# Planner costs for full fp32 products in the w_in stage, and two gMLP value blocks ahead of their inputs

## The chip, the cores and the metric

One NeuronCore of one Trainium2 chip runs the kernel. The metric is the device time of one execution in microseconds (us). TensorE is called PE, VectorE DVE, ScalarE ACT, GpSimd POOL; SP is the queue of SyncE, which issues nearly all DMAs here. An engine works through its own instructions strictly in the order of the program and waits at an instruction whose inputs are not there.

## What is computed

One layer over 640 tokens (512 latent, 128 context), model width 2048, all in fp32. Cut to what matters:

```python
h = rmsnorm(x, norm1_g) * (1.0 + sc1) + sh1
p = h @ w_in                                  # 2048 -> 3360 + 2048
o_a, s_fin = rwkv7_bidir(shift(p[..., :C_SHIFT]), s0)      # 8 pairs of heads
u, v = split(gelu(p[..., C_SHIFT:]), 2)       # gMLP, 8 groups of 128 channels
v = layernorm(v) * ln_g + ln_b                # per token and group
o_b = u * (w_spatial[g] @ v + b_spatial[g])   # per 128-token chunk
x = x + g1 * (concat(o_a, o_b) @ w_out)
# then: rmsnorm, SwiGLU (w_ffn_gate, w_ffn_up, w_ffn_down), final rmsnorm
```

## The kernel before

**The w_in stage** (some 150 to 1016 us of the profile) multiplies `h` by `w_in`, a block of 128 output channels at a time. A block has four pieces of 512 input channels, each split into two fp32r parts `hi` and `lo`, and takes 96 products of 128x128 by 128x320: the *wide* products, written as `big<-h_hi,hi`, `big<-h_lo,hi` and `big<-h_hi,lo`. What comes out of a block goes through a generator of its own: `take_r`, `take_v`, `take_k` for the pairs of heads, `take_gv` for a gMLP value block, `take_gu` for the gMLP gate block of the same group. These issue many *small* PE instructions: transposes, fp32 products on the whole array, and products on quarters or sixteenths of the array (64x64 and 32x32 modes), plus the `pm` products of the modulation (128x32 mode).

The order on every engine in this stage is a list written when the kernel is built. `Lister` keeps a clock for each engine, prices every instruction with a formula (`Op.__init__`, lines 106 to 130), and appends to each engine what its planned clock can start next; on PE it takes a small instruction when it has been ready long enough or two are ready, else the wide task (`pick`). The prices decide the order only; no wait is computed from them.

**Blocks and queues.** `block()` lines up the blocks pair by pair; the gMLP blocks are put behind the pairs by `GORD = (0, 1, 1, 2, 2, 3, 3, 8)`: groups 3 to 7 follow the last pair. All `take_gv` and `take_gu` generators stand in one queue, `qB`, and run one after the other.

**A value block** (`take_gv`, from line 946): gelu of 128x640, a transpose `pw` of `w_spatial`, five transposes `pvt`, then a chain on DVE, ACT and POOL: mean `gmn`, subtraction, square `gsq`, `gva`, `grs`, and three multiplications and additions on the tile `vt`. **A gate block** (`take_gu`): gelu (square and tanh on ACT in `gq`, three steps on DVE), five products `psp<-wspT,vt`, two additions `sp`, a last multiplication, and a store into `d_o`.

**The recurrence stage** follows (lines 1294 to 1580). Its order is set by the framework's scheduler, not by the list. It loads `gl` and `gr` (the gate's input), transposes tiles of `x` (`pxT<-ident,x1T`, two rounds per tile through one PSUM bank, each copied out by ACT), loads `o_b` back (`ol<-d_o`, cast to `oh`), multiplies it by half of `w_out` (`big<-oh,hi` and so on, called w_out products here), and runs the chunk recurrences of the pairs in between (`swap`, `w_ps`, `u_ps`, `s_ps`, `y_ps`). The single PSUM bank of the transposes is one that the w_in stage's last `psp` used.

Of the kernel before, what the change touches and what calls it, by code (L numbers as in the profile page):

```python
# [10 lines left out]
F32 = mybir.dt.float32  # L11
F32R = mybir.dt.float32r
# [7 lines left out]
P = 128  # L20
# [3 lines left out]
NT = T // P  # L24
# [7 lines left out]
DA = 1024  # L32
NPAIR = DA // P
CSH = 3360
# [16 lines left out]
TOGETHER = 2  # L51
PATIENCE = 2.0
SLACK = 1.0
NREC = 8
CHK = (3, 3, 4, 4, 4, 4)
POOLK = (3,)
# [32 lines left out]
class Op:  # L89
# [14 lines left out]
    def __init__(self, eng, name, fn, args, kw):  # L104
        ap = lambda x: hasattr(x, "tensor")
        self.eng, self.run = eng, lambda: fn(*args, **kw)  # L106
        outs = [x for x in (kw.get("out", args[0] if args else None), kw.get("accum_out")) if ap(x)]
        rest = [x for k, x in [*enumerate(args), *kw.items()] if ap(x) and not any(x is y for y in outs)]
        self.writes, self.reads = {x.tensor.name for x in outs}, {x.tensor.name for x in rest}
        self.stored = {x.tensor.name for x in outs if x.space == DRAM}  # L110
        n = max(math.prod(x.shape[1:]) for x in outs + rest)
        self.bytes, self.tiling = 0, None
        if name == "dma_start":
            run = min(self.run_of(x) for x in (outs[0], args[1]))
            self.bytes = 4 * math.prod(outs[0].shape) * min(4.0, max(1.0, 64 / run))
            self.cost = 0.5 if eng == "SP" else 0.65
        elif eng == "DVE":
            self.cost = 0.16 + 1e-3 * n * self.RATE.get(name, 1.03)
        elif eng == "ACT":
            self.cost = 0.2 + 0.83e-3 * n + 0.09 * any(ap(kw.get(k)) for k in ("scale", "bias"))  # L120
        elif eng == "POOL":
            self.cost = 0.05 + 1e-3 * n if name == "memset" else 0.2 + 0.185 * n
        else:
            lhs, rhs = args[1], args[2]
            q = lambda m: 32 if m <= 32 else 64 if m <= 64 else P
            self.tiling = (q(lhs.shape[0]), q(lhs.shape[1])) if name == "matmul" else (P, P)
            n = math.prod(rhs.shape[1:])
            share = P * P // (self.tiling[0] * self.tiling[1])
            least = {1: 0.108, 4: 0.05, 16: 0.016}[share] if self.tiling != (P, 32) else 0.08
            self.cost = max(least, (n / 2400 + 0.0133 if rhs.dtype == F32R else n / 1200) / share)  # L130


class Kept:
# [78 lines left out]


class Task:
    def __init__(self, gen, prio):
        self.gen, self.prio, self.item, self.over = gen, prio, None, False
        self.step()

    def step(self):
# [11 lines left out]
class Lister:  # L231
# [7 lines left out]
        self.wide = Task(wide, 0)  # L239
        self.tasks.append(self.wide)  # L240

    def add(self, gen, prio):
        self.tasks.append(Task(gen, prio))

    def ready(self, ops):
        e, r = ops[0].eng, 0.0
# [36 lines left out]
    def pick(self, eng, tasks):  # L283
        now = self.clock[eng]
        c = [(self.ready(t.item), t.rank(), i, t) for i, t in enumerate(tasks)]
        if eng == "PE":
            small = [x for x in c if x[3] is not self.wide and x[0] + SLACK * (x[3].item[0].tiling != self.tiling or self.tiling == (P, P)) <= now]
            wide = [x for x in c if x[3] is self.wide and x[0] <= now]
            full = [x for x in small if x[3].item[0].tiling == (P, P)]
            if full and self.tiling == (P, P):  # L290
                return now, min(full, key=lambda x: x[1])[3]
            if small and self.tiling != (P, P):
                same = [x for x in small if x[3].item[0].tiling == self.tiling]
                return now, min(same or small, key=lambda x: x[0])[3]
            if small and (not wide or len(small) >= TOGETHER or now - min(small)[0] >= PATIENCE):
                return now, min(small)[3]
            if wide:
                return now, self.wide
        start = min(max(now, x[0]) for x in c)
        return start, min((x for x in c if max(now, x[0]) <= start), key=lambda x: (x[1], x[0], x[2]))[3]  # L300
# [18 lines left out]
def flow_step(ctx: ExitStack, tc, x_prompt, x_sample, state_rwkv, c, c_ctx, w_mod, b_mod,  # L319
# [43 lines left out]
    def bcast(col, like):  # L363
        for _ in like.shape[2:]:
            col = col.unsqueeze(2)
        return col.to_broadcast(list(like.shape))
# [45 lines left out]
    wide = [0]  # L412
# [182 lines left out]
    bk, bp, gs, bz = (hp.enter_context(tc.tile_pool(name=n, bufs=1)) for n in ("bk", "bp", "gs", "bz"))  # L595
# [38 lines left out]
    class Mixer:  # L634


        def __init__(self):
            self.q, self.left, self.budget, self.done, self.apart = [], 0.0, 0.0, 0, False
            self.hold = 0

        def add(self, gen, cost):
            self.q.append(gen)
            self.left += cost
# [42 lines left out]
    bk, bp, gs, bz, db = Kept(bk), Kept(bp), Kept(gs), Kept(bz), Kept(db, 2)  # L686
# [163 lines left out]
    wl, done = {}, {"zv": 0}  # L850
# [85 lines left out]
    def gelu2(xx):  # L936

        sq = bp.tile([P, T], F32, tag="u2", name="gq", bufs=1)
        yield oS.activation(sq, xx, AF.Square)
        yield oV.tensor_scalar(sq, sq, GC1, 1.0, op0=ALU.mult, op1=ALU.add)  # L940
        yield oV.tensor_mul(sq, sq, xx)
        yield oS.activation(sq, sq, AF.Tanh, scale=GC0)
        yield oV.scalar_tensor_tensor(out=xx, in0=sq, scalar=1.0, in1=xx, op0=ALU.add, op1=ALU.mult)
# [3 lines left out]
    def take_gv(vv, g, read):  # L947
        lng, lnb, wsp = (gs.tile([P, P], F32, tag=n, name=n) for n in ("lng", "lnb", "wsp"))
        yield oQ.dma_start(lng, gmlp_ln_g[0, g].partition_broadcast(P))
        yield oQ.dma_start(lnb, gmlp_ln_b[0, g].partition_broadcast(P))  # L950
        yield oQ.dma_start(wsp, w_spatial[0, g])
        yield from gelu2(vv)
        yield slots.free
        pw = slots.tile([P, 4, P], F32, "pw")
        yield oT.transpose(pw[:, 0, :], wsp, ident)
        wspT = gs.tile([P, P], F32, name="wspT")
        yield oS.copy(wspT, pw[:, 0, :])
        slots.done(pw)
        vt = bp.tile([P, NT, P], F32, tag="vt2", name="vt2", bufs=1)
        yield from turned(vv, vt, "pvt2")  # L960
        bc = lambda ap: ap.unsqueeze(2).to_broadcast([P, NT, P])
        mn = gs.tile([P, NT], F32, name="gmn")
        yield oV.tensor_reduce(out=mn, in_=vt, axis=AX.X, op=ALU.add)
        yield oV.tensor_scalar_mul(mn, mn, 1.0 / P)
        yield oV.tensor_tensor(out=vt, in0=vt, in1=bc(mn), op=ALU.subtract)
        sq = bp.tile([P, NT, P], F32, tag="u2", name="gsq", bufs=1)
        yield oS.activation(sq, vt, AF.Square)
        va = gs.tile([P, NT], F32, name="gva")
        yield oV.tensor_reduce(out=va, in_=sq, axis=AX.X, op=ALU.add)
        yield oV.tensor_scalar(va, va, 1.0 / P, 4.0 * LN_EPS, op0=ALU.mult, op1=ALU.add)  # L970
        rstd = gs.tile([P, NT], F32, name="grs")
        yield oG.tensor_tensor(out=rstd, in0=va, in1=bcast(mhalf, va), op=ALU.pow)
        yield oV.tensor_tensor(out=vt, in0=vt, in1=bc(rstd), op=ALU.mult)
        fb = lambda ap: ap.unsqueeze(1).to_broadcast([P, NT, P])
        yield oV.tensor_tensor(out=vt, in0=vt, in1=fb(lng), op=ALU.mult)
        yield oV.tensor_tensor(out=vt, in0=vt, in1=fb(lnb), op=ALU.add)
        vts[g] = (vt, wspT)
# [149 lines left out]
    qA, qB, qS, qM, qT, qR, qX, qZ = [], [], [], [], [], [], [], []  # L1127
    blocks = [(FIRST[i], lambda h, read, i=i, n=n: low_rank(h, 24 + i, n), qA) for i, n in enumerate((P, P, 32))]

    def block(col, fn, i, q):  # L1130
        blocks.append((col, lambda pr, read: fn(pr, i, read), q))

    g = 0
    for p in range(NPAIR):
        block(P * p, take_r, p, qR)
        block(2 * DA + P * p, take_v, p, qR)
        block(DA + P * p, take_k, p, qA)
        while g < GORD[p]:
            block(CSH + DA + P * g, take_gv, g, qB)
            block(CSH + P * g, take_gu, g, qB)  # L1140
            g += 1
    pieces = [(b, q) for b in range(len(blocks)) for q in range(4)]
    N0 = 4 * len(FIRST)
    parts, praw = {}, []
# [150 lines left out]
    with ExitStack() as ph:  # L1295
# [26 lines left out]
        def flip(cc):  # L1322

            a, b = cc[0], NCH + cc[1]
            return slice(a, b + 1, b - a)
# [10 lines left out]
        def load_next():  # L1336
            if todo:
                _, p, ctx_, step = todo.pop(0)
                r = rw.tile([P, 2, REC], F32, tag="rec", name="rec", bufs=NREC)
                nc.sync.dma_start(r, d_S[p].rearrange("p d c f -> p (d c) f")[:, flip(seqs[ctx_][step])])  # L1340
# [207 lines left out]
        m3.run(4.0 + 8 * 4.0)  # L1548
        for _ in range(NREC - 4):
            load_next()  # L1550
# [26 lines left out]
    t1, t2 = slice(0, HALF), slice(HALF, T)  # L1577
# [629 lines left out]
```

## Time and profile before

| what | value |
|---|---|
| median of 3 runs | 3248.59 us (3248.25 to 3256.41) |
| the profiled execution | 3247.45 us; span of its instructions 3244.2 us |
| mean granted clock of TensorE | 0.983 |
| PE busy | 3107.5 us, 96% of the span |
| DVE, ACT, POOL busy | 72%, 45%, 39% |
| DMA | 553 MB moved, 170 GB/s over the span |

In the rows further down, a stretch is given as start:end and its length, then busy time and number of instructions of PE, PEld (weight loads, beside PE), DVE, ACT and POOL, the clock granted to TensorE as a share of its full speed, the mean busy share of the DMA engines and GB/s. A timeline row is start, duration, engine, line, operation, output<-input, shapes, how many, and in brackets the idle time of the engine before it and what ended that.

PE is the engine that is nearly always busy. The places where it stands still, or runs at half its clock, are where time can be won or lost.

### The profile page before, as it was taken

How to read it: one execution, taken by the hardware profiler on the slowest of the kernel's cores; microseconds unless marked ns; L12 is line 12 of the kernel's file. 1: busy time of each engine (PE TensorE's matmuls, PEld its weight loads, DVE VectorE, ACT ScalarE, POOL GpSimd, SP SyncE). 2: the span in 40 equal slices, each digit the busy share in tenths (PEclk: the TensorE clock that was granted, in tenths of full speed). 3: DMA queues.
4: the chain of work that ended last, by engine and by line, in shares of the span. 5: the costliest groups of instructions: out<-in, count | busy, mean ns of one | idle time of the engine just before them, and what ended most of it. 6: DMA issues, size and time to landing. Idle time of an engine off the chain costs nothing. (4 is left out here: it accounts for less than half of the span.)

```text
span 3244.2 us, 73519 instructions
## 1 busy us (share of the span) xinstructions
PE 3107.5 (96%) x28828; PEld 2877.5 (89%) x28828; DVE 2333.3 (72%) x4073; ACT 1446.0 (45%) x3161; POOL 1260.9 (39%) x1082
## 2 busy tenths in 40 slices
PE   5899999999998999898999999999999999999996
PEld 3698888889886877788999999999999999999986
DVE  4456767767666666547977877877877777777787
ACT  3244554555543333345644444444444444444365
POOL 0001222222220122301365666566666645555543
PEclk8899999999997999999999999999999999999998
DMA  8768788887896777455434434434433354554353
GB/s 319 254 183 237 212 224 212 237 233 192 230 233 191 215 222 226 136 152 175 123 108 130 125 105 128 127 107 123 123 116 118 110 180 151 160 160 141 110 170 119
DMA packets 741922, 553.00 MB, mean 170 GB/s; under 512 B 141688, under 2 KB 674184, under 8 KB 732744
## 3 DMA queue, kind: packets, MB, share of 16 engines
q1 hardware_dynamic: 729256, 534.62, 55.5%
q0 software_dynamic: 9984, 13.13, 1.7%
q8 instruction: 226, 3.70, 0.5%
q14 instruction: 120, 0.98, 0.1%
q10 hardware_dynamic: 2336, 0.57, 0.1%
HBM read 438.77 MB, written 111.69 MB: 170 GB/s over the span
## 5 line engine op out<-in xcount | busy, mean ns | idle before, releaser
L1819 PE MATMUL P<-xo,lo 128*128 128x320 f32 x2352 | 727.1, 309 | 3.5 <-DVE lo L1636 3.5
L1818 PE MATMUL P<-xo,hi 128*128 128x320 f32 x2352 | 727.6, 309 | 0.0
L1817 PE MATMUL P<-xo,hi 128*128 128x320 f32 x2352 | 727.6, 309 | 0.0
L1636 DVE TENSOR_TENSOR lo<-raw,hi 128x512 fp32r<-128x512 f32 x532 | 514.4, 974 | 162.0 <-ACT hi L1635 159.6
L1635 ACT CAST hi<-raw 128x512 fp32r<-128x512 f32 x532 | 330.2, 622 | 505.6 <-PE P L1818 435.6
L1819 PEld LDWEIGHTS P<-xo,lo 128*128 128x128 f32 x2352 | 441.6, 188 | 4.3 <-DVE lo L1636 4.2
L1818 PEld LDWEIGHTS P<-xo,hi 128*128 128x128 f32 x2352 | 442.3, 188 | 0.0
L1817 PEld LDWEIGHTS P<-xo,hi 128*128 128x128 f32 x2352 | 442.3, 188 | 0.0
L1730 POOL TENSOR_TENSOR raw<-raw 128x512 f32<-128x512 f32 x252 | 413.6, 1645 | 13.6 <-DVE lo L1636 0.6
L106 PE MATMUL big<-h_hi,hi 128*128 128x320 f32 x1280 | 417.8, 326 | 0.9 <-ACT praw L1209 0.9
L1819 PE MATMUL P<-xd,lo 128*128 128x320 f32 x1232 | 384.4, 312 | 16.8 <-DVE lo L1636 16.2
L106 PE MATMUL big<-h_lo,hi 128*128 128x320 f32 x1280 | 394.1, 308 | 0.0
L106 PE MATMUL big<-h_hi,lo 128*128 128x320 f32 x1280 | 394.1, 308 | 0.0
L1817 PE MATMUL P<-xd,hi 128*128 128x320 f32 x1232 | 381.9, 310 | 5.1 <-ACT hi L1635 3.0
L1818 PE MATMUL P<-xd,hi 128*128 128x320 f32 x1232 | 380.7, 309 | 0.0
L1730 POOL TENSOR_TENSOR t<-raw 128x512 f32<-128x512 f32 x84 | 129.5, 1542 | 454.8 <-DMA raw<-in_w_ffn_up_dram 407.5
L1635 ACT CAST hi<-rawd 128x512 fp32r<-128x512 f32 (+1 forms) x288 | 168.7, 588 | 237.9 <-PE P L1818 198.5
L106 PEld LDWEIGHTS big<-h_hi,hi 128*128 128x128 f32 x1280 | 240.7, 188 | 32.6 <-issue 25.9
L1819 PEld LDWEIGHTS P<-xd,lo 128*128 128x128 f32 x1232 | 231.2, 188 | 25.6 <-DVE lo L1636 25.6
L106 PEld LDWEIGHTS big<-h_lo,hi 128*128 128x128 f32 x1280 | 240.7, 188 | 1.2
L106 PEld LDWEIGHTS big<-h_hi,lo 128*128 128x128 f32 x1280 | 240.1, 188 | 0.0
L1817 PEld LDWEIGHTS P<-xd,hi 128*128 128x128 f32 x1232 | 231.4, 188 | 8.6 <-ACT P L2116 4.8
(370 smaller groups left out, 6268.3 us busy)
## 6 DMA issues: line engine op xcount, KB each, us to landing
wt<-in_w_mod_dram SPq DMA_DIRECT2D x96, 1024.0 KB
raw<-in_w_ffn_gate_dram SPq DMA_DIRECT2D x182, 256.0 KB
raw<-in_w_ffn_up_dram SPq DMA_DIRECT2D x182, 256.0 KB
rec<-d_S SPq DMA_DIRECT2D x80, 576.0 KB
raw<-in_w_in_dram SPq DMA_DIRECT2D x172, 256.0 KB
rawd<-in_w_ffn_down_dram SPq DMA_DIRECT2D x128, 256.0 KB
raw<-in_w_out_dram SPq DMA_DIRECT2D x96, 256.0 KB
xd<-d_os SPq DMA_DIRECT2D x66, 320.0 KB
```

What stands on the lines that cost most here:

```text
L106: self.eng, self.run = eng, lambda: fn(*args, **kw)
L1635: S.copy(hi[:, 0:nk], raw[:, 0:nk])
L1636: V.tensor_sub(lo[:, 0:nk], raw[:, 0:nk], hi[:, 0:nk].bitcast(F32))
L1730: G.tensor_tensor(out=o[:, 0:nk], in0=p[:, 0:nk], in1=q[:, 0:nk], op=ALU.subtract)
L1817: TE.matmul(ps, hi[:, k, :], xk[:, 0, :], start=f, stop=False)
L1818: TE.matmul(ps, hi[:, k, :], xk[:, 1, :], start=False, stop=False)
L1819: TE.matmul(ps, lo[:, k, :], xk[:, 0, :], start=False, stop=l)
```

## The change

It does three things. The price of a PE instruction in the planner is split in three: transposes at least 0.109 us; fp32r products as before, but no longer divided by the share of the array; plain fp32 products at twice the columns' price, at least 0.22 us on the whole array, 0.015 to 0.08 in the small modes and 0.028 off the diagonal. A wait limit of its own can be given to each task (`patience`; every task is added with the old value, and the three new constants `PACE`, `PATM`, `PATT` are read nowhere). And the last two groups of gMLP, 6 and 7, change places in the line of blocks: value 6, value 7, gate 6, gate 7, where value 6, gate 6, value 7, gate 7 stood; so that both values can be alive, group 7 keeps its `vt` and `wspT` in tiles that the pairs have finished with.

```diff
-            self.cost = max(least, (n / 2400 + 0.0133 if rhs.dtype == F32R else n / 1200) / share)
+            if name == "transpose":
+                self.cost = max(0.109, n / 1200)
+            elif rhs.dtype == F32R:
+                self.cost = max(0.108, n / 2400 + 0.0133)
+            else:
+                where = kw.get("tile_position")
+                least = {1: 0.22, 4: 0.05 if self.tiling != (P, 32) else 0.08, 16: 0.015}[share]
+                self.cost = max(least if not where or where[0] == where[1] else 0.028, n / 600 / share)
...
-            if small and (not wide or len(small) >= TOGETHER or now - min(small)[0] >= PATIENCE):
+            if small and (not wide or len(small) >= TOGETHER or any(now - x[0] >= x[3].patience for x in small)):
...
-        wspT = gs.tile([P, P], F32, name="wspT")
+        wspT = (bk if g == 7 else gs).tile([P, P], F32, tag="wlr" if g == 7 else "wspT", name="wspT", bufs=1)
...
-        vt = bp.tile([P, NT, P], F32, tag="vt2", name="vt2", bufs=1)
+        if g == 7:
+            yield lambda: done["zv"] == NPAIR
+        vt = bp.tile([P, NT, P], F32, tag="t2" if g == 7 else "vt2", name="vt2", bufs=1)
...
-            block(CSH + DA + P * g, take_gv, g, qB)
-            block(CSH + P * g, take_gu, g, qB)
-            g += 1
+            both = (g, g + 1) if g == 6 else (g,)
+            for u in both:
+                block(CSH + DA + P * u, take_gv, u, qB)
+            for u in both:
+                block(CSH + P * u, take_gu, u, qB)
+            g += len(both)
```

PE at the end of the w_in stage, before. The last wide product stands above the first row; `pw`, `pvt` and `psp` are those of group 7:

```order
L106 MATMUL pw<-ident,wsp 128x128
L106 MATMUL pvt_13759<-ident,praw 128x128 x4
L106 MATMUL pvt_13765<-ident,praw 128x128
L106 MATMUL psp<-wspT,vt_13758 128x128 x5
L1537 MATMUL pxT<-ident,x1T 128x128 x4
L1351 MATMUL swap<-I_68,s_13887 64x64 x4
L1537 MATMUL pxT<-ident,x1T 128x128
L1411 MATMUL w_ps<-ST,rec 64x64 x4
L1377 MATMUL y_ps<-ST,rec 64x64
L1537 MATMUL pxT<-ident,x1T 128x128 x4
```

The same place now; the first three rows are the last wide products:

```order
L109 MATMUL big<-h_hi,hi 128x320
L109 MATMUL big<-h_lo,hi 128x320
L109 MATMUL big<-h_hi,lo 128x320
L109 MATMUL psp<-wspT,vt_13592 128x128 x5
L1551 MATMUL pxT<-ident,x1T 128x128 x25
L1365 MATMUL swap<-I_68,s_13887 64x64
L1551 MATMUL pxT<-ident,x1T 128x128 x4
L1365 MATMUL swap<-I_68,s_13887 64x64 x3
L1425 MATMUL w_ps<-ST,rec 64x64 x2
L1551 MATMUL pxT<-ident,x1T 128x128
```

The transposes of value block 7 moved ahead: 99 wide products now stand between the last `pvt` and the last five `psp`, where none stood. Five tiles of `x` are transposed before the first recurrence step, where that step began after the first round.

ACT at the same place, before, from the last cast of a w_out weight to the first copy of a transposed `x`:

```order
L398 CAST hi<-raw 128x512
L106 ACTIVATE gq<-gq 128x640
L106 COPY wspT<-pw 128x128
L1266 CAST oh<-ol 128x640
L106 COPY vt_13758<-pvt_13759 128x512
L106 COPY vt_13758<-pvt_13765 128x128
L1307 CAST gh<-gl 128x640
L106 ACTIVATE gsq<-vt_13758 128x640
L1312 CAST gq<-gr 128x640
L106 ACTIVATE gq<-praw 128x640
L106 ACTIVATE gq<-gq 128x640
L1538 COPY x1T<-pxT 128x512
```

and now, from the last copy out of the wide products' PSUM on:

```order
L109 COPY praw<-big 128x320
L109 ACTIVATE gq<-praw 128x640
L1321 CAST gh<-gl 128x640
L109 ACTIVATE gq<-gq 128x640
L1326 CAST gq<-gr 128x640
L1552 COPY x1T<-pxT 128x512
L1552 COPY x1T<-pxT 128x128
```

The chain of value 7 is gone from here. The cast of `gl`, a tile that the stage behind loads, now stands between the square and the tanh of the last gate's gelu. The load of `gl`, which takes the place of `h`, is now held by the last wide product itself; before, it stood on SP behind a load that waits for `pw`, the next product after the last wide one.

## Rows read from the trace of the kernel before

**Rows 1.** Busy time of each engine in four stretches (windows)
```profile
201.00:1016.00 815.00, 808.91 (x11010) 711.62 (x11008) 560.03 (x1182) 407.99 (x891) 188.78 (x298) 1.00 0.81 217
1016.00:1035.00 19.00, 4.20 (x17) 3.28 (x16) 13.85 (x22) 7.40 (x14) 2.18 (x2) 0.58 0.85 267
1035.00:1057.00 22.00, 21.68 (x168) 16.95 (x169) 9.92 (x26) 9.45 (x27) 0.00 (x0) 0.59 0.57 174
1057.00:1366.00 309.00, 308.17 (x4451) 248.90 (x4451) 202.94 (x638) 108.39 (x490) 77.00 (x103) 1.00 0.68 206
```

**Rows 2.** Timeline of PE, 1016 to 1057 us: start, duration, work [idle <-releaser]
```profile
1016.12 0.30 PE L106 MATMUL pw<-ident,wsp 128*128 128x128 f32 x1
1019.25 1.30 PE L106 MATMUL pvt<-ident,praw 128*128 128x128 f32 x5 [2.83 <-DVE praw L106]
1031.87 2.47 PE L106 MATMUL psp<-wspT,vt 128*128 128x128 f32 x10 [11.32 <-DVE vt L106]
1035.20 1.12 PE L1537 MATMUL pxT<-ident,x1T 128*128 128x128 f32 x4 [0.86 <-DVE sp L106]
1036.99 0.47 PE L1537 MATMUL pxT<-ident,x1T 128*128 128x128 f32 x1
...
1038.02 1.11 PE L1537 MATMUL pxT<-ident,x1T 128*128 128x128 f32 x4
...
1050.99 0.90 PE L1279 MATMUL big<-oh,hi 128*128 128x320 f32 x2
...
1056.89 0.41 PE L1279 MATMUL big<-oh,hi 128*128 128x320 f32 x1
```

**Rows 3.** Timeline of DVE, the last steps of value 7 and gate 7
```profile
1021.16 0.82 DVE L106 TENSOR_REDUCE gmn<-vt 128x5 f32<-128x640 f32 x1 [0.88 <-ACT vt L106]
...
1030.90 0.82 DVE L106 TENSOR_TENSOR vt<-vt,lnb 128x640 f32<-128x640 f32 x1
...
1033.34 0.82 DVE L106 SCALAR_TENSOR_TENSOR praw<-gq,praw 128x640 f32<-128x640 f32 x1
1034.25 0.89 DVE L106 TENSOR_TENSOR sp<-psp,bsp 128x512 f32<-128x512 f32 x2
```

**Rows 4.** Timeline of ACT at the same place
```profile
1022.28 0.72 ACT L1307 CAST gh<-gl 128x640 fp32r<-128x640 f32 x1 [1.15 <-DMA gl<-d_gs]
...
1032.49 0.74 ACT L106 ACTIVATE gq<-gq 128x640 f32<-128x640 f32 x1 [5.24 <-DVE gq L106]
```

**Rows 5.** Timeline of the SP queue: when each DMA is issued
```profile
1016.83 0.49 SPq L1306 DMA_DIRECT2D gl<-d_gs  x1
...
1036.03 0.34 SPq L106 DMA_DIRECT2D d_o<-praw  x1
```

**Rows 6.** Timeline of PE in the recurrence stage at full clock
```profile
1087.45 0.45 PE L1411 MATMUL w_ps<-SN,rec 64*64 64x64 f32 x8
1087.83 0.69 PE L1382 MATMUL y_ps<-rec 128*64 128x64 f32 x16
1088.45 0.45 PE L1377 MATMUL y_ps<-SN,rec 64*64 64x64 f32 x8
```

**Rows 7.** Timeline of PE in the w_in stage, into the 32x32 mode and out
```profile
970.86 0.30 PE L106 MATMUL big<-h_hi,lo 128*128 128x320 f32 x1
971.10 0.89 PE L106 MATMUL pblk<-TB,A__1111 32*32 32x32 f32 x80
971.91 0.41 PE L106 MATMUL big<-h_hi,hi 128*128 128x320 f32 x1
972.16 0.31 PE L106 MATMUL big<-h_lo,hi 128*128 128x320 f32 x1
972.31 0.31 PE L106 MATMUL big<-h_hi,lo 128*128 128x320 f32 x1
```

**Rows 8.** Waits of PE between 170 and 1017 us: total, times, longest (us)
```profile
PE pblk L106 <- issue: 2.0, 2, 1.4
PE pm L106 <- DMA wt<-in_w_mod_dram: 1.5, 2, 0.8
PE pmm L106 <- ACT Z L106: 1.1, 1, 1.1
PE pG L106 <- issue: 1.0, 1, 1.0
```

More of the change, by code (lines that the diff above doesn't have):

```diff
@@ L53 @@
 SLACK = 1.0
+PACE = 2.0
+PATM = 2.0
+PATT = 2.0
 NREC = 8
@@ L128, in __init__ @@
             share = P * P // (self.tiling[0] * self.tiling[1])
-            least = {1: 0.108, 4: 0.05, 16: 0.016}[share] if self.tiling != (P, 32) else 0.08
-            self.cost = max(least, (n / 2400 + 0.0133 if rhs.dtype == F32R else n / 1200) / share)
+            if name == "transpose":
[6 more added lines that the diff above has]
+                self.cost = max(least if not where or where[0] == where[1] else 0.028, n / 600 / share)
 class Kept:
@@ L214, with __init__ @@
 class Task:
-    def __init__(self, gen, prio):
-        self.gen, self.prio, self.item, self.over = gen, prio, None, False
+    def __init__(self, gen, prio, patience=0.0):
+        self.gen, self.prio, self.patience, self.item, self.over = gen, prio, patience, None, False
         self.step()
@@ L240, in __init__, with add @@
         self.tasks.append(self.wide)
-    def add(self, gen, prio):
-        self.tasks.append(Task(gen, prio))
+    def add(self, gen, prio, patience=PATIENCE):
+        self.tasks.append(Task(gen, prio, patience))
     def ready(self, ops):
```

## The prediction

> **What bounds the kernel now.** I read the busy time by stretches first [rows 1]. In the w_in stage, from 201 to 1016 us, PE works 808.91 of 815 us at a granted clock of 1.00: its share of full speed, so 2.4 GHz. In the recurrence stage behind it, from 1057 to 1366 us, it works 308.17 of 309 us, also at 1.00. Between the two lie 41 us in which it is different: PE does 4.20 us of work in the first 19 us, and in the next 22 us it is full but the granted clock is 0.59 on average. So there are only two things to win: the 6 us in which PE stands in the long stage, and the hole between the stages. Everything else is work that PE has to do.
>
> The timeline of PE shows the hole [rows 2]. After the last wide product come `pw` at 1016.12, five `pvt`, the five `psp` (ten records) and the first transposed tile of `x` at 1035.20; ahead of them PE is idle for 2.83, 11.32 and 0.86 us. The 11.32 us are the chain of value 7 on DVE, from `gmn` at 1021.16 to the end of `lnb` at 1031.72; then gate 7's last two steps run, and `sp` frees the PSUM bank of the transposes [rows 3]. From 1035.20 PE is full, but not at its full speed: five transposes take 1.12 and 0.47 us, the w_out products 0.41 to 0.45 us apiece at first. They come to stay at 1056.89.
>
> **The hole, up to the first transpose of x.** The change puts 99 wide products between the last `pvt` and the last `psp`. At 0.15 us each (972.16 to 972.31 [rows 4]) they take 14.9 us; the chain from the end of `pvt` (1020.55) to the end of `lnb` takes 11.2 us. So `vt` of group 7 is ready some 3.7 us before it is wanted, and the 2.83 and 11.32 us of idle time go. What is late next is gate 7. Its tanh stood ready in time before; now ACT has the cast of `gl` ahead of it, and the load of `gl` can start only when the last wide product is done with `h`. Before, from the issue of that load to the start of the cast it took 5.45 us (1016.83 [rows 5] to 1022.28 [rows 6]). From t0, the end of the wide products (1016.12 before), I count: issue 0.3 (an estimate from SP's 0.49 us per issue), load 5.45, cast 0.72, tanh 0.74 [rows 6], the step on `praw` 0.82, `sp` 0.89 [rows 3], 0.1 for the handing over: t0 + 9.0. Before it was 1035.20 - 1016.12 = t0 + 19.1. **Term A: -10.1.** If the load took no time beyond the square on ACT it would be 5.4 less; if it queued as the w_out weights' loads do at that moment, when DMA is 0.85 busy [rows 1], some 3 more (my estimate: half of 5.45 again).
>
> The Trainium skill, page "DMA: Bandwidth & Descriptors", section "Anatomy of one DMA", fits one transfer by about 2.0 us and its bytes at 436 GB/s, for the queue of the other kind of descriptors. By our estimate from that page a load of 327,680 bytes takes 2.75 us, and the sum would be 2.7 us lower; the trace has 5.45 us for this very load, and I take that.
>
> **From there to the w_out products.** Before, 1035.20 to 1056.89: 21.7 us, in which PE also does recurrence steps of the first pair. Now five tiles of transposes come first. A tile repeats after 2.82 us (1035.20 to 1038.02 [rows 2]): each half waits until ACT has copied the other out of the one bank. Five tiles are 14.1 us; `swap`, the sixth tile and the first steps make some 3.5 us more to the first w_out product, and from the first to the steady ones it was 5.9 us (1050.99 to 1056.89) at the lower clock. 23.5 us. **Term B: +1.8.**
>
> **What slides behind.** In exchange fewer recurrence products lie in the hole: by the order, 24 `y`, 16 `u`, 16 `w` and 8 `s` (in records of the trace) now come later, in a stage where PE is full. There eight of them take 0.38 us (1087.45 to 1087.83) or 0.31 (sixteen `y` in 0.62, 1087.83 to 1088.45 [rows 7]): 40 by 0.38/8 is 1.9, 24 by 0.31/8 is 0.9. One tile of transposes less remains there, about 0.6 (half of 1.12 + 0.47, or a little under, as the clock is double). **Term C: +2.2.**
>
> **The w_in stage itself.** PE's instructions are the same in number. `pw` and the five `pvt` of group 7 now lie among the wide products at full clock: half of 0.30 and 1.30, so 0.8 at most, I take +0.7. The array changes mode 420 times up to the last `psp`, where it was 411. Into the 32x32 mode a wide product took 0.24 us to the next start and out of it 0.25, where 0.15 is usual (970.86 to 971.10, 971.91 to 972.16 [rows 4]): 0.1 each way, nine more cost +0.9. The Trainium skill says more than that: by "TensorEngine Tiling (Array Packing)", "Key Properties", a change of mode drains TensorE, and it speaks against every added one. The trace agrees that there is a price; the page has no figure for it.
>
> The waits of PE in this stage are 2.0, 1.5, 1.1 and 1.0 us [rows 8], 5.6 in all. The new prices move every small instruction by a little, and nothing in the trace says which waits will meet. The bounds are that all vanish (-5.6) or that as many come again (+5.6); I take 0, since the wide products, which stand ready on PE throughout, cover any shift. **Term D: +1.6.** DVE (560 of 815 us), ACT and POOL keep slack there; their new orders cost nothing as long as PE has wide products to put between.
>
> **The rest.** From the middle of the recurrence stage on PE's order is the same word for word; up to there the changes of mode go from 518 to 509. **Term E: 0**, bounds -0.9 and +0.9. The patience part does nothing: every task has the old value, so the new condition is the old one, and the three constants are read nowhere.
>
> Sum: -10.1 + 1.8 + 2.2 + 1.6 = **-4.5**. The profiled execution took 3247.45 us, so 3242.95; the median of the runs shown is 1.1 above it. I say 3243 us.
>
> **Rivals.** 0.3%, or 9.7 us, is about what a measurement of this kernel can tell from no change, so "faster" begins at 3238.9.
>
> *The waits of the list go too.* Prices nearer to the truth put the small products where their inputs really are. For it: two of the four waits are `pblk` and `pmm` [rows 8], full fp32 products whose price changes. Against it: the two largest are ended by nothing that the order of PE sets (an issue, a load). All gone: -4.5 - 5.6 = -10.1, 3237 us. Chance 0.2.
>
> *The clock keeps up.* From 1016 to 1057 the granted clock is 0.58 and 0.59, a mean between the two levels 2.4 and 1.2 GHz; before it fell, PE had stood for 2.83 us and then 11.32. Now PE stands once, for some 7 us, less its five `psp`. If the clock stays at 2.4 GHz, the five tiles lose half of their PE time (1.59 each, so 4.0) and the last 5.9 us shrink to about 3.5: -4.5 - 6.4 = -10.9, 3236.5. Against it: even 2.83 us of standing was followed by transposes of 0.26 us apiece (five in 1.30). Chance 0.1.
>
> *Small products come too early.* The slower side. The planner now believes that a small fp32 product is dearer: so in its plan PE takes longer than it does, and the true PE may come to small products before their inputs are there. One such wait took 1.1 us (`pmm` on `Z` [rows 8]). The blocks of the eight pairs, two directions each, go through the same steps; if each met one such wait it would be 16 by 1.1 = 17.6, so +13.1, 3260.5. It decides from 13 waits on (13 by 1.1 = 14.3 = 9.7 + 4.5). For it: the list has no slack on PE (99% busy), so each wait counts in full. Against it: the list takes a small product only when it has been ready for some time or two are, and that is slack. Chance 0.08.
>
> *The change doesn't do what it says.* The chain of value 7 could still end the wait if the 99 wide products were gone before it ended; then part of 11.32 us stays. It has 3.7 us of slack, and it would give 3243 to 3248: inside the forecast's side. Chance 0.05.
>
> **How the numbers follow.** The forecast has 0.57, the rivals 0.2, 0.1, 0.08 and 0.05. The lower end of the range joins the first rival with the quicker load (3237 - 2.7, about 3234); the upper end is the forecast with the waits doubled, E at its bound and the queued load (3243 + 5.6 + 0.9 + 3 = 3252.5). Faster by over 0.3%: the two rivals that do it, 0.3. Slower: 0.08 and a little that several bounds meet, 0.09. Within: 0.61.
>
> **What would show it.** Right: no wait of PE for `vt` at the end of the w_in stage; one idle stretch of 6 to 8 us instead of 15 us in three; the first `pxT` 9 us after the last wide product, released by `sp`, and ACT's tanh directly behind the cast of `gl`; the first steady w_out products some 32 to 33 us after the last wide product (40.8 before); PE busy about 810 us up to there as before; the rest of the program as long as it was, but for 2 us. Wrong: a wait for `vt` of several us; a stage up to the last wide product that is longer or shorter by over 5 us; a granted clock of 1.00 across the hole; the first `pxT` released by something other than gate 7.

## The result, and the profile after

The changed kernel takes 3260.03 us (median of 16 runs, 3253.09 to 3270.96), the kernel before in the same jobs 3249.28 us (16 runs): a ratio of 1.0028, with a 95% interval of 1.002 to 1.0036. It is slower by some 9 to 11 us, where the prediction said 3243 us, with a range of 3234 to 3252.5 and a chance of 0.09 for slower. The profiled execution took 3259.9 us, its span is 3257.7 us (before 3244.2). These two profiles lie 13.5 us apart, a little more than the medians, 10.8.

One correction to the prediction's text: three of its group numbers are interchanged. Where it says rows 4 the rows stand in group 7 (the changes of mode), its rows 6 are group 4 (ACT), and its rows 7 are group 6 (the recurrence at full clock).

The busy time by stretches, cut at the places that answer to those of [rows 1]:

```profile
201.00:1033.59 832.59, 816.00 (x11015) 715.05 (x11015) 569.06 (x1193) 414.38 (x897) 188.60 (x300) 0.99 0.80 213
...
1033.60:1041.00 7.40, 1.41 (x13) 1.22 (x11) 4.60 (x8) 3.77 (x6) 0.00 (x0) 0.92 0.83 269
1041.00:1057.00 16.00, 10.71 (x42) 6.47 (x42) 3.10 (x6) 5.50 (x12) 0.00 (x0) 0.50 0.98 301
1057.00:1063.00 6.00, 5.83 (x36) 4.48 (x36) 3.15 (x6) 2.50 (x5) 0.00 (x0) 0.50 0.04 13
```

The w_in stage now lasts until 1033.59 us, 17.6 us longer: PE stands for 16.6 us in it (832.59 - 816.00) where it stood for 6, and its busy time grew by some 7 us as well. The timeline of PE at the end of the stage answers to [rows 2]:

```profile
1033.59 0.30 PE L109 MATMUL big<-h_hi,lo 128*128 128x320 f32 x1
1033.74 1.27 PE L109 MATMUL psp<-wspT,vt 128*128 128x128 f32 x10
1041.11 1.11 PE L1551 MATMUL pxT<-ident,x1T 128*128 128x128 f32 x4 [6.10 <-DVE sp L109]
1042.90 0.48 PE L1551 MATMUL pxT<-ident,x1T 128*128 128x128 f32 x1 [0.68 <-ACT x1T L1552]
1043.73 1.12 PE L1551 MATMUL pxT<-ident,x1T 128*128 128x128 f32 x4 [0.35 <-ACT x1T L1552]
...
1054.22 1.12 PE L1551 MATMUL pxT<-ident,x1T 128*128 128x128 f32 x4
```

The wait for `vt` is gone, and the first `pxT` comes 7.4 us after the wide products (1033.74 to 1041.11) where it was 19.1. So the hole did what was forecast. The SP queue and ACT show why it is even a little shorter than the 9.0 us of the prediction; they answer to [rows 5] and [rows 4]:

```profile
1033.93 0.33 SPq L1320 DMA_DIRECT2D gl<-d_gs  x1
```

```profile
1037.76 0.72 ACT L1321 CAST gh<-gl 128x640 fp32r<-128x640 f32 x1 [2.21 <-DMA gl<-d_gs]
1038.39 0.73 ACT L109 ACTIVATE gq<-gq 128x640 f32<-128x640 f32 x1
```

The load of `gl` took 3.83 us from issue to cast (1033.93 to 1037.76), not 5.45. So the row of before was too much by 1.6 us, which is the whole difference from 9.0. The 2.75 us of the estimate by the Trainium skill, page "DMA: Bandwidth & Descriptors", section "Anatomy of one DMA" (a fit for DMAs that GpSimd issues; this one is issued by SyncE), were too little by 1.1 us.

The loss is in the list. Its waits, from 201 us to the last wide product, answer to [rows 8], which add up to 5.9 us with one of 0.3 more:

```profile
PE pm L109 <- DMA wt<-in_w_mod_dram: 5.3, 3, 3.0
PE pG L109 <- issue: 3.5, 2, 2.0
PE pXT L109 <- DVE GA L109: 2.7, 1, 2.7
PE pblk L109 <- issue: 2.6, 2, 1.9
PE pw L109 <- DMA wsp<-in_w_spatial_dram: 1.9, 1, 1.9
PE pT L109 <- issue: 0.4, 1, 0.4
```

They are 16.4 us in ten waits, spread over the stage (the seven longest at 306, 450, 517, 610, 825, 855 and 976 us), not at the two blocks that changed places. That is +10.5. And a wait can cost more than its idle time, as the timeline at two of them and the stretches behind three show:

```profile
306.29 1.89 PE L109 MATMUL pm<-wt,cT 128*2 128x512 f32 x8 [3.03 <-DMA wt<-in_w_mod_dram]
...
976.00 1.04 PE L109 MATMUL pm<-wt,cT 128*2 128x512 f32 x8 [1.91 <-DMA wt<-in_w_mod_dram]
```

```profile
306.30:308.00 1.70, 1.70 (x8) 0.10 (x8) 0.00 (x0) 0.00 (x0) 0.00 (x0) 0.50 1.18 332
308.00:310.00 2.00, 2.00 (x13) 1.89 (x10) 1.22 (x3) 0.00 (x0) 0.00 (x0) 0.67 0.74 198
...
517.60:519.00 1.40, 1.40 (x6) 1.40 (x7) 1.34 (x4) 0.27 (x1) 0.55 (x2) 0.50 0.99 352
519.00:521.00 2.00, 2.00 (x9) 2.00 (x9) 1.97 (x4) 1.24 (x3) 0.00 (x0) 0.52 0.95 279
...
854.70:856.00 1.30, 1.28 (x8) 1.26 (x9) 1.27 (x4) 0.32 (x2) 0.00 (x0) 0.78 0.93 232
856.00:859.00 3.00, 3.00 (x14) 2.96 (x13) 2.83 (x8) 2.47 (x5) 0.00 (x0) 0.53 1.15 341
```

Eight records of the same product take 1.89 us after a wait of 3.03 us and 1.04 us at 976 us, after one of 1.91. In the stretches shown the granted clock is 0.50 to 0.78, so PE runs partly or wholly at 1.2 GHz, behind the two longest waits (3.03 and 2.69 us) and behind one of 1.93 us at 855 us, the wait of `pw` for its load. Length by lost share of the clock, that is 0.85 + 0.66 + 0.70 + 0.96 = 3.2 us behind the first two and 0.29 + 1.41 = 1.7 us behind the third: 4.9 us, which the view counts as busy time of PE. Behind the waits of 2.03 and 1.91 us the clock stayed at 1.00, so the length of a wait alone doesn't tell.

### The profile page after: what moved, and what is told of

Read it like the earlier page. It is cut to its first block, busy times and chain, and to the rows that moved or that the text cites. A ratio compares the mean times of both kernels' runs of the same rounds, so it can differ in the third digit from the quotient of the medians.

```text
span 3257.7 us, 73537 instructions
## 1 busy us (share of the span) xinstructions
PE 3117.7 (96%) x28828; PEld 2881.5 (88%) x28828; DVE 2341.9 (72%) x4073; ACT 1449.3 (44%) x3161; POOL 1259.4 (39%) x1082
```

## The experiments

Every kernel was timed in five rounds beside the kernel before (4 executions of e4, 5 of e3 and e16, 7 to 12 of the others, 16 of the changed kernel). A number that recurs is the *planned time*: what the planner's own clock of PE shows at the last wide product. It is 812 us with the old prices and 864 us with the new, where the first one stands at 4. From the first to the last of these products the plan of before has 808 us and the trace 866; the changed kernel's plan has 859, its trace 884. Theory A: the old prices made PE look 7% faster than it is (866 by 808), and this was a margin for the loads and the other engines; the new prices are nearer to the truth and take it away. Theory B: before has a good list by choice, and any other would be worse. Theory C: the order of the blocks did it.

| kernel | planned us | waits of PE in the list, us | last wide at, us | median us | ratio to before, 95% |
|---|---|---|---|---|---|
| before | 812 | 5.9 | 1015.8 | 3249.28 to 3251.16, by job | |
| e2 | 812 | 8.0 | 1018.5 | 3248.03 | 0.999 (0.9981 to 0.9999) |
| e5 | 814 | 7.1 | 1024.5 | 3248.49 | 0.9997 (0.9989 to 1.0006) |
| e6 | 814 | 5.6 | 1016.2 | 3251.4 | 1.0001 (0.9991 to 1.0011) |
| e11 | 836 | 14.5 | 1032.4 | 3256.82 | 1.0027 (1.0015 to 1.0038) |
| e3 | 838 | 11.5 | 1026.2 | 3262.94 | 1.0041 (1.0027 to 1.0055) |
| after | 864 | 16.4 | 1033.6 | 3260.03 | 1.0028 (1.002 to 1.0036) |
| e1 | 864 | 16.8 | 1034.0 | 3261.2 | 1.003 (1.0021 to 1.0039) |
| e7 | 862 | 16.7 | 1035.6 | 3261.24 | 1.0027 (1.0016 to 1.0039) |
| e8 | 862 | 19.6 | 1039.9 | 3266.64 | 1.0044 (1.0029 to 1.0059) |
| e4 | 912 | 23.3 | 1051.4 | 3283.29 | 1.0102 (1.0088 to 1.0116) |
| e9, DMA x 1.064 | 864 | 9.0 | 1025.4 | 3257.92 | 1.002 (1.0009 to 1.003) |
| e10, engines x 1.064 | 861 | 8.7 | 1020.4 | 3252.1 | 1.0003 (0.9994 to 1.0011) |
| e13, engines x 1.10 | 861 | 7.0 | 1016.9 | 3245.58 | 0.9988 (0.9979 to 0.9996) |
| e12, e2 and late gates | 812 | 7.7 | 1015.6 | 3242.16 | 0.9971 (0.996 to 0.9982) |
| e14, after and late gates | 864 | 18.3 | 1036.2 | 3255.11 | 1.0012 (1.0002 to 1.0023) |
| e15, before and late gates | 812 | 8.9 | 1019.8 | 3246.27 | 0.9987 (0.9975 to 0.9999) |
| e16, e13 and late gates | 861 | 4.2 | 1015.9 | 3237.07 | 0.9961 (0.9949 to 0.9974) |

Waits and the last wide product come from one profile of each kernel; the ratio is from all runs. Four pairs of kernels have the same list in this stage (before and e15, e2 and e12, after and e14, e13 and e16): their waits differ by 0.3 to 3.0 us, so a difference of that size says nothing about a list. In the kernels with late gates the loads and casts of `gl` and `gr` come later (last group below).

**The two halves of the change: e1 and e2.** e1 is before with the new `self.cost` lines alone, e2 the changed kernel with the old ones:

```diff
-            if name == "transpose":
-                self.cost = max(0.109, n / 1200)
...
+            least = {1: 0.108, 4: 0.05, 16: 0.016}[share] if self.tiling != (P, 32) else 0.08
+            self.cost = max(least, (n / 2400 + 0.0133 if rhs.dtype == F32R else n / 1200) / share)
```

> The new prices alone, the block order of before. Theory A (the new prices take away a margin: planned time up to the last wide product is 812 us with the old prices and 864 with the new, where the trace of before has 866 us for the same list, so PE used to come late to its small products and now comes on time): the last wide product some 17 us later than before, the 11 us wait for vt still there, so about 3262 to 3266 us. Theory C (the block order did the harm): within 2 us of before. Theory B (any reordering of the list makes it longer or shorter by chance): as A, since the list is nearly the same as in the changed kernel.

> The block order alone, the old prices. Theory A and theory B: the list as before up to the last two blocks, waits of PE in it some 6 us, the last wide product within 3 us of before; the hole shorter by some 5 us net as in the changed kernel: 3242 to 3246 us, faster than before by 3 to 6. Theory C: the last wide product 15 to 18 us later, about 3260 us.

The prices alone bring the whole loss (1.003), the block order alone is slightly faster than before (0.999). Theory C falls. e2 gained less than was expected (3248.03 us for 3242 to 3246): with the old prices the list still puts value 7 so late that the last `psp` waits for `vt`, 6.41 us in place of 11.32, as PE's timeline of e2 shows:

```profile
1018.61 1.27 PE L109 MATMUL psp<-wspT,vt 128*128 128x128 f32 x10
1026.30 2.47 PE L109 MATMUL psp<-wspT,vt 128*128 128x128 f32 x10 [6.41 <-DVE vt L109]
1035.21 1.11 PE L1545 MATMUL pxT<-ident,x1T 128*128 128x128 f32 x4 [6.44 <-DVE sp L109]
```

For e1 the text before the run expected the 11 us wait for `vt` to stay, as the order of the blocks is the old one. It did not. With the new prices the list puts the `pvt` of value 7 among the wide products by itself:

```profile
1027.01 0.27 PE L106 MATMUL pvt<-ident,praw 128*128 128x128 f32 x1
1036.82 2.47 PE L106 MATMUL psp<-wspT,vt 128*128 128x128 f32 x10 [2.50 <-DVE J L1310]
1041.30 1.11 PE L1543 MATMUL pxT<-ident,x1T 128*128 128x128 f32 x4 [2.01 <-DVE sp L106]
```

The first `pxT` stands 7.1 us behind the last wide product (at 1034.01 us) in e1 and 16.6 us in e2 (1018.61 to 1035.21). So between these two it is the prices that close the hole as well as bring the waits, and beside the new prices the block order gives nothing that the times can tell (1.003 and 1.0028).

**More and less of the price: e3 and e4.** One line behind the prices of the changed kernel:

```diff
+            self.cost *= 0.97
```

(1.06 in e4.)

> The changed kernel with every price of PE times 0.97 (planned time to the last wide product 838 us, half way back to before). Theory A: half of the margin is back, so waits of PE in the list fall from 16 to about 11 us, and the run is 4 to 6 us shorter than the changed kernel, about 3254 us. Theory B: no relation; waits anywhere from 5 to 17 us.

> The changed kernel with every price of PE times 1.06 (planned time 912 us, longer than PE truly needs). Theory A: PE runs ahead of its plan, waits grow to 25 us or more, and the run is 10 us or more longer than the changed kernel, above 3270 us. Theory B: no relation; waits anywhere from 5 to 17 us.

The time of e4 went where theory A sent it, only further: 3283.29 us. Its waits came to 23.3 us, a little under the 25 expected, and 11.3 of them are for other engines' results, where the changed kernel has 2.7. The first rows:

```profile
PE pw L109 <- DMA wsp<-in_w_spatial_dram: 4.6, 1, 4.6
PE pXT L109 <- DVE GA L109: 3.9, 1, 3.9
PE pG L109 <- DVE X L109: 2.8, 2, 2.4
```

e3 is a miss: the waits of its profile are the 11 us that were expected, but that execution is the fastest of its five, and the median is no better than that of the changed kernel.

**Other lists at the same prices: e5 to e8.** These tell theory A from B. One constant of the planner moves by 2 to 5%, which makes another list without touching the margin: with the old prices `SLACK = 1.05` (e5) and 0.0163 for sixteenths (e6), with the new ones `SLACK = 0.95` (e7) and `PATIENCE = 2.1` (e8); the edit of e6 against e2, for instance:

```diff
-            least = {1: 0.108, 4: 0.05, 16: 0.016}[share] if self.tiling != (P, 32) else 0.08
+            least = {1: 0.108, 4: 0.05, 16: 0.0163}[share] if self.tiling != (P, 32) else 0.08
```

> Old prices and the new block order, with SLACK 1.05 in place of 1.0: another list with nothing changed in its margin (planned last wide product 814 us, 279 runs of wide products against 263 in before, 379 changes of mode against 374). Theory A (margin of the prices): waits of PE in the list stay at 5 to 9 us as in before and e2; with 16 more runs some 2 to 3 us longer than e2, 3249 to 3252 us. Theory B (before has a good list by choice, and any other is worse): waits 11 us or more, last wide product at 1028 us or later, 3256 us or more.

> Old prices and the new block order, with 0.0163 in place of 0.016 for products of sixteenths of the array: another list with the same margin (planned last wide product 814 us, 270 runs, 382 changes of mode). Theory A: waits 5 to 9 us, 3248 to 3251 us. Theory B: waits 11 us or more, 3255 us or more.

> The changed kernel with SLACK 0.95: another list with the new prices (planned last wide product 862 us, 267 runs, 374 changes of mode). Theory A: waits 13 to 20 us as in the changed kernel, since the margin is as small; 3256 to 3264 us. Theory B: anything from 6 to 20 us.

> The changed kernel with PATIENCE 2.1: another list with the new prices (862 us, 260 runs, 375 changes of mode). Theory A: waits 13 to 20 us, less some 2 us for fewer runs; 3255 to 3262 us. Theory B: anything from 6 to 20 us.

The lists fall into two groups by their prices: with the old ones (before, e2, e5, e6) waits of 5.6 to 8.0 us and times within 0.1% of before, with the new ones (after, e1, e7, e8) 16.4 to 19.6 us and 0.27 to 0.44% more, whatever the list. Theory B falls. e8 took 3266.64 us, more than the 3255 to 3262 expected; the other three came within 1 us of theirs. Waits that end with "issue" are part of these sums, and no input that comes late explains them; without them the groups stand apart as well, 2.9 to 6.9 us against 8.6 to 16.9.

The waits are not all that a list costs. In e5 the last wide product comes 8.6 us later than in before, with only 1.2 us more of waits; PE's busy time there is 816.18 us for 808.75. Three stretches have a lower granted clock (0.76 to 0.79 over 7 or 8 us), behind waits of 0.8 and 0.6 us at 615 us, 2.1 at 725 and 2.5 at 977; by the same count that is 5.0 of the 7.4 us. Its time equals that of before because the hole is shorter (the first `pxT` at 1034.82 us, where before has 1035.20).

**Giving the margin back another way: e9, e10, e13.** The new prices of PE stay; the planner counts the others longer. In e9 all terms of a DMA but the cost of its issue are larger by 1.064, in e10 and e13 those of the instructions of DVE, ACT and POOL by 1.064 and 1.1. From e13:

```diff
-            self.cost = 0.16 + 1e-3 * n * self.RATE.get(name, 1.03)
+            self.cost = 1.1 * (0.16 + 1e-3 * n * self.RATE.get(name, 1.03))
```

(ACT and POOL in the same way.)

> The changed kernel, whose planner now also counts every DMA 1.064 times as long (864/812, so that a DMA stands to PE in the plan as it did in before); planned last wide product 864 us, 277 runs, 387 changes of mode. Theory A1 (the margin that was lost is the one of loads): waits of PE for DMA and for issue fall from 14 us to 4 to 8, last wide product 8 us earlier, some 3252 us, 2 to 4 of these us given back for 18 more runs. Theory A2 (the margin lost is that of all engines alike): little change, 3256 to 3262 us. Neither: 3262 us or more.

> The changed kernel, whose planner counts every instruction of DVE, ACT and POOL 1.064 times as long and DMA as before; 861 us, 273 runs, 377 changes of mode. Theory A1: waits for DMA stay (12 to 16 us), 3257 to 3262 us. Theory A2: waits for engines fall from 2.7 us to under 1, and DMA and issue waits fall as well, since what a DMA moves comes from an engine: 3252 us.

> The changed kernel, whose planner counts every instruction of DVE, ACT and POOL 1.10 times as long; planned last wide product 861 us, 261 runs, 371 changes of mode. Theory A (the price of PE against the other engines' sets the waits): waits of PE in the list 9 us or less and the last wide product at 1021 us or earlier, as in e10; 3246 to 3252 us. If e10 was one lucky list: waits 14 us or more and 3257 to 3263 us.

The waits fall to 9.0, 8.7 and 7.0 us, and the time to 1.002, 1.0003 and 0.9988. The waits of e13:

```profile
PE pw L109 <- DMA wsp<-in_w_spatial_dram: 1.9, 2, 1.7
PE pW L109 <- DMA Z<-d_vt: 1.6, 3, 0.7
PE pmm L109 <- DVE sp L109: 1.5, 1, 1.5
PE pm L109 <- DMA wt<-in_w_mod_dram: 1.1, 1, 1.1
PE big L109 <- issue: 0.9, 1, 0.9
```

So the new prices do no harm as such; what counts is PE's price against that of the others. That theory is A, in the form called A2. A1, that loads alone lack the margin, is borne out by half: in e9 the waits for DMA and for issue fell to 7.1 us and the last wide product came 8.2 us earlier, as A1 said, but the time, 3257.92 us, stayed where A2 had it.

**One price: e11.** `pm` products at the old price, the others new:

```diff
-                self.cost = max(least if not where or where[0] == where[1] else 0.028, n / 600 / share)
+                self.cost = max(least if not where or where[0] == where[1] else 0.028, n / (1200 if self.tiling == (P, 32) else 600) / share)
```

> The changed kernel with the old price of the pm products (0.107 us in place of 0.213; 240 of them take 58 us in the trace, 0.24 each): planned last wide product 836 us, half of the margin back. Theory A: waits 8 to 13 us and 3252 to 3257 us, between before and the changed kernel. If the pm price alone is to blame, as for before: waits under 8 us and 3250 us.

3256.82 us is at the upper end of what was expected, its waits, 14.5 us, are above it, and its interval overlaps that of the changed kernel. With e3 it says that half of the margin does not bring half of the time back. Why is open. A part of it for e11 may lie behind the list: in its profile the last `psp` waits 6.41 us (the view puts it down to ACT's `gq`), and the first `pxT` comes 16.6 us behind the last wide product, where it is 7.4 in the changed kernel.

**The end of the stage: e12, e14, e15, e16.** The load and casts of `gl` and `gr` are needed only when the first pair is finished; they move from the start of the recurrence stage into its loop:

```diff
-        nc.sync.dma_start(gl.bitcast(F32), d_gs[0:P])
-        S.copy(gh, gl.bitcast(F32))
...
+        def gates():
+            nc.sync.dma_start(gl.bitcast(F32), d_gs[0:P])
+            S.copy(gh, gl.bitcast(F32))
...
         for hop in range(hops):
+            if hop == 6:
+                gates()
```

> The block order alone with the old prices (e2), and the load and casts of gl and gr moved from the start of the recurrence stage to its seventh hop. The tanh of gate 7 then follows the square on ACT without the cast of gl: the first pxT 5 to 6 us behind the last wide product in place of 7.4, so 1.5 to 2.5 us less than e2, if the casts later cost nothing. If the wait of pxT is set by something else (the store of praw, the loads on SP), no change.

> The changed kernel with the loads and casts of gl and gr at the seventh hop. The list and its waits stay (last wide product at 1032 to 1036 us). If the gain of e12 belongs to the move (SP's queue reaches the state and the recurrence's records 3 us sooner, ACT the tanh): 5 to 8 us less than the changed kernel, 3252 to 3255 us. If it needs the old prices' order: 0 to 2 us less.

> Before, with the loads and casts of gl and gr at the seventh hop. The wait for vt of value 7 (11 us) stays, but the recurrence steps of the first pair can run into it, as they do in e12. If the gain belongs to the move: 4 to 8 us less than before, 3243 to 3246 us. If the block order is needed for it: within 2 us of before.

> e13 with the late loads: waits in the list as in e13, the hole as short as in e14 (first pxT 5 to 6 us behind the last wide product). If both add: 5 to 8 us less than e13, 3240 to 3246 us.

The medians fall by 4 to 9 us: e2 to e12 5.9, after to e14 4.9, before to e15 4.0, e13 to e16 8.5. The move helps by itself; it isn't the block order that makes it. e14 and e15 came within 0.3 us of what was expected, e16 3 us below it. Expected for e12 was 1.5 to 2.5 from ACT alone, with the first `pxT` 5 to 6 us behind the last wide product; it came 15.2 us behind. What gives the rest was not tested by itself, as loads and casts were moved together. The traces point to SP: in e13 its queue holds five issues between the stage and the loads of the first recurrence,

```profile
1017.28 0.33 SPq L1320 DMA_DIRECT2D gl<-d_gs  x1
1017.66 1.87 SPq L1325 DMA_DIRECT2D gr<-d_gs  x4
1019.65 0.38 SPq L1354 DMA_DIRECT2D rec<-d_S  x1
1024.93 0.34 SPq L109 DMA_DIRECT2D d_o<-praw  x1
1025.32 1.59 SPq L1354 DMA_DIRECT2D rec<-d_S  x3
1026.95 1.40 SPq L1359 DMA_DIRECT2D s<-in_state_rwkv_dram  x2
```

and three records and both states fall behind the store of `praw`, which waits for the last gate. In e16 all four records go ahead of that store, and the states follow 7.4 us behind the last `psp` (1015.99 to 1023.41) where it was 9.9 (1017.09 to 1026.95). The same queue and then PE:

```profile
1016.18 2.30 SPq L1356 DMA_DIRECT2D rec<-d_S  x4
1022.73 0.33 SPq L109 DMA_DIRECT2D d_o<-praw  x1
1023.41 0.91 SPq L1361 DMA_DIRECT2D s<-in_state_rwkv_dram  x2
```

```profile
1015.99 1.28 PE L109 MATMUL psp<-wspT,vt 128*128 128x128 f32 x10
1021.85 0.66 PE L1553 MATMUL pxT<-ident,x1T 128*128 128x128 f32 x4 [4.58 <-DVE sp L109]
...
1027.97 0.47 PE L1367 MATMUL swap<-I,s 64*64 64x64 f32 x2 [0.21 <-DMA s<-in_state_rwkv_dram]
```

The same two instructions of PE in e13:

```profile
1024.04 1.12 PE L1551 MATMUL pxT<-ident,x1T 128*128 128x128 f32 x4 [5.67 <-DVE sp L109]
...
1038.21 0.69 PE L1365 MATMUL swap<-I,s 64*64 64x64 f32 x8
```

The recurrence's `swap` starts at 1027.97, among the first transposes, where in e13 it starts at 1038.21. So PE has more to do between the transposes, and its granted clock is back at 1.00 sooner, as the 26 us from the first `pxT` on show, e13 above and e16 below:

```profile
1024.04:1050.04 26.00, 20.41 (x100) 14.21 (x100) 7.55 (x14) 8.65 (x20) 0.00 (x0) 0.53 0.67 208
...
1021.85:1047.85 26.00, 23.55 (x150) 19.75 (x151) 10.59 (x23) 9.88 (x20) 0.00 (x0) 0.74 0.82 259
```

From the first `pxT` to the 301st w_out product it is 98.1 us in e16 and 104.5 in e13, so 6.4 of the 8.8 us between the two profiles lie there. e15 shows nothing of the kind: its clock over the like 26 us is 0.63 where before has 0.65, in the slowest of its twelve executions, and where its 4.0 us come from stays open. e16 is the best version found, 0.9961 of before (0.9949 to 0.9974): both parts of the change kept, with a margin in the planner's prices and the gates' loads moved.

## Why the prediction was wrong

**The hole, term A: right.** -10.1 was forecast, -11.7 measured (7.4 in place of 19.1 us), by the steps that were named: no wait for `vt`, the gate's tanh behind the cast of `gl`, `pxT` released by `sp`. The difference of 1.6 is the load of `gl`; the 2.7 us that the lower end of the range takes off for a quicker load are in no run. The prediction did not part the change's two halves here; by e1 and e2 the new prices close the hole (7.1 us), and the block order alone leaves 16.6.

**Terms B and C: right in sign, too small.** From the first `pxT` to the 301st w_out product it was 96.8 us before (1035.20 to 1132.04) and is 103.9 now (1041.11 to 1145.05): +7.1 against +4.0. Up to the steady w_out products (1056.89 before, 1067.06 now) it is 26.0 us in place of 21.7, +4.3, so most of what is missing belongs to term B. The five tiles cost a little less than was said (2.62 us apiece, 1041.11 to 1043.73, for 2.82), but the clock stayed low longer: 0.50 up to 1063 us, 22 us after the first `pxT`, where it was 18 (a mean of 0.59 over 22 us [rows 1]). PE waits for ACT's copies nine times there and is busy 10.71 of 16 us.

**Term D: the step that failed.** "I take 0, since the wide products, which stand ready on PE throughout, cover any shift", and so +1.6. It was +17.6. A wide product covers a small one only as long as the list has it ahead of the small one; on the chip PE goes strictly by the list, and when the small one's input isn't there, the wide products queue behind it. What decides is how long before its use the list believes an input ready, against the error of the plan. The old prices made the planned PE 7% too fast, so inputs were as a rule there earlier than planned, against PE. With the new prices the plan is short by only 25 us of 884, waits included, and ten small products met a wait. That it is PE's price against the others' is shown by the lists with the same prices (e2, e5, e6; e1, e7, e8) and by those that raise the others' prices instead (e10, e13); why a given product met its wait was not followed up. The sum goes: 10.5 of more waits, 4.9 of lower clock behind three of them, 0.7 for group 7's transposes and 0.9 for nine changes of mode (both as forecast, neither measured alone); some 0.6 us are not assigned. The upper bound of the range allowed the waits to double, +5.6, and put no price on the clock behind a wait.

**Term E and the patience part: as forecast.** From the 301st w_out product to the end the two profiles differ by 0.5 us.

**The rivals.** "Small products come too early" had a chance of 0.08 and gave 3260.5 us; it is what happened. Its reason was half wrong: PE's plan did not become longer than the truth, it stopped being much shorter. Its price was for 16 waits of 1.1 us; there were ten of 1.6 on average, four of them for a load and five ended by "issue", not by an input. That its 3260.5 us meets the measured 3260.03 is luck: it rests on terms A, B and C as forecast and has no loss of clock. "The waits of the list go too", 0.2, rested on the idea that truer prices make a better list, and the runs show the contrary. "The clock keeps up" is refuted: 0.50 from 1041 to 1063 us. It also read the fall before wrongly: there the granted clock is 1.00 from 1016 to 1019 us and 0.50 to 0.51 from 1019 on, so one stop of 2.83 us had gone before the fall, not the 11.32 as well. "The change doesn't do what it says" did not happen: no wait for `vt`.

The evidence for the right side was there: the trace of before gives 866 us for a list that its plan runs through in 808, so that plan was optimistic for PE, and the change took that away while the other engines' prices and the loads' stayed as they were.

## What to carry to other kernels

In a list that is fixed when the kernel is built, a wrong price can be a safety margin. Before a price is corrected, compare the plan's own total with the trace, for every engine; a truer price for one engine must come with a margin for what it waits for (here 10% on the other engines, e13). And at the seam between two stages look at what the in-order queues hold in front of the first loads of the next stage: moving five issues on SP, and their casts on ACT, to where their data is needed gained 4 to 9 us.

## What the runs showed of the hardware

- A wait inside full work can cost PE more than its idle time: behind waits of 3.03, 2.69 and 1.93 us the granted clock was 0.50 to 0.78, which cost 1.5 to 1.7 us each, and the eight `pm` records took 1.89 us in place of 1.04. Behind waits of 2.03 and 1.91 us it was 1.00.
- Waits that end with "issue" (3.0 us before, 6.5 in the changed kernel, 0.9 in e13, 0.6 in e16) come inside long runs of small products or right behind one: at 450 us of the changed kernel behind the sixteenth of 32 `pG`, at 610 us behind 40 `pblk`. What PE waits for there the profile doesn't show, and no run was made for it.
- Run-to-run scatter of one kernel is 10 to 20 us here (before: 3245.23 to 3256.41 in 16 executions), so a single profile can mislead, as that of e3 does.
